# Attention in a two-layer hybrid block: each unit's output is read out of PSUM in the next unit's opening, added in place, with a second buffer for its scale

## The chip, the cores and the metric

The kernel runs on one core of one Trainium2 chip. The metric is the device time of one execution in microseconds (us); lower is better. Everything is fp32; products that need more than one pass of the matrix engine are made from a rounded high part and a remainder (`hi`, `lo`).

## The reference

Two layers work on 1024 latent tokens behind 256 context tokens, width 1024. Each layer normalises the tokens, makes one joint projection, and feeds two mixers: eight heads of latent attention (key width 96, value width 64) and four heads of a gated delta rule in both directions. One output projection and an MLP follow. What matters here is the attention:

```
def mla_attend(q, k, v):
    ...
    def block(qi):
        s = jnp.einsum('bqhd,bkhd->bhqk', qi, k).astype(jnp.float32) * scale
        p = jax.nn.softmax(s, axis=-1).astype(v.dtype)
        return jnp.einsum('bhqk,bkhd->bqhd', p, v)
...
    attn_l = mla_attend(q, jnp.concatenate([kc, k], axis=1), jnp.concatenate([vc, v], axis=1))
    gdn_l, gdn_c = gdn_mix(feat_l, feat_c, gdn_norm_g, not last)
    x = x + g1 * (jnp.concatenate([attn_l, gdn_l], axis=-1) @ w_out)
```

Latent queries read all 1280 keys, context queries the 256 context keys, and the last layer has no context queries.

## The kernel before, in words

Each layer has three stages: projections (`stage1`), the two mixers (`stage2`), and output projection with MLP (`stage3`). `stage2` writes the steps of the delta rule between the attention's units (L801 to L813).

**A unit** is one head, one block of tokens and one half of it, 256 queries: `keys` (L859) lists 40 in layer 0 and 32 in layer 1, 72 in all. Unit i runs the front of query tile i and the back of query tile i-1, interleaved by `PATTERN`.

- `front` computes the scores (names `St`, `S`), copies them out of PSUM with their row maximum (L908), applies the exponential (L926, ScalarE, which also sums the rows), and inverts the two sums of a row (L930, tile `rinv`). The 256 inverted sums lie one per partition; they are needed along the free axis, so a DMA writes them to DRAM (L933) and a second one reads them back, broadcast to 64 partitions (L935, tile `rb`). `rb` has one buffer.
- `back` transposes the exponentials (L955, `pt`), splits them into `ph` (L958, ScalarE) and `pl` (L959, VectorE), and multiplies by the values (L947). The values' high part stands in 64 columns of the weights and their remainder in the other 64, so the product `o` has two halves of 64 partitions that must be added. Tiles `o` alternate between the two halves of one PSUM bank (`o2`, L887).
- At the end of `back` the result is taken out: ScalarE copies the lower half (L969, `oh`), VectorE adds the upper (L971, `ob`), GpSimd multiplies by the inverted sums (L972), and a DMA writes the result to DRAM (L973, tensor `cat`).

**Loads.** `plan` (L861) says in which unit the next head's keys, values and queries are fetched. `prepare(i)`, called as unit i begins, issues these loads through a staging tile `raw` (L834) and splits what the unit before fetched (L839 ScalarE, L841 GpSimd). The splits are put behind `amark`, the last exponential written so far (L879): `issue_after` keeps ScalarE's part of them behind that instruction in ScalarE's order.

**What sets the order.** A scheduler works the program over when it is built: it orders each engine's instructions by written order, priority, and its own estimate of when operands and buffers are ready. All DMAs of this stage are issued by SyncE (SP) from one queue in this order, the loads of the delta rule among them (L1028, L1030, L1032 and L1083). An instruction at the head of an engine's order that has to wait holds up all that stand behind it there.

Of the kernel before, what the change touches and what calls it, by code (L numbers as in the profile page):

```python
# [8 lines left out]
F32 = mybir.dt.float32  # L9
# [3 lines left out]
ALU = mybir.AluOpType  # L13
# [4 lines left out]
P = 128  # L18
# [97 lines left out]
class K:  # L116
# [700 lines left out]
    def attention(self, l, last, ap, psA, psO):  # L817
        nc = self.nc
        ap, ap1, ap2 = ap
# [39 lines left out]
        keys = [(h, b, half) for h in range(H_A) for b in ([1, 2] if last else [0, 1, 2]) for half in range(1 if b == 0 else 2)]  # L859

        plan = {}  # L861
        for h in range(H_A):
            i = min(j for j, k in enumerate(keys) if k[0] == h)
# [5 lines left out]
        wait = []  # L869

        def prepare(i):
            if i == 0:
                for j in sorted(plan):
                    if j < 0:
                        for f, *a in plan[j]:
                            f(*a)()
            todo, wait[:] = list(wait), [f(*a) for f, *a in plan.get(i, [])]
            if todo:
                with self.tc.issue_after(self.amark.ins):  # L879
                    for x in todo:  # L880
                        x()

        state = {}
        self.mark = None


        o2 = psO.tile([P, 2, 256], F32, name="o2")  # L887
        nb = [0]

        def front(h, b, half):  # L890
            prepare(keys.index((h, b, half)))
            t = cur[h]
            qh, ql = cur[h, b]
            nk = NCTX if b == 0 else NT
            nch = (nk + 511) // 512
            sm = self.small.tile([P, 2], F32, tag="sm", name="sm", bufs=3)
            mx = self.small.tile([P, 2, nch], F32, tag=f"mx{nch}", name="mx", bufs=3)
            mn = self.small.tile([P, 2], F32, tag="mn", name="mn", bufs=3)

            def scores(s, i, c0, c1):  # L900
                q = slice(half * 256 + i * P, half * 256 + (i + 1) * P)
                self.mm3(s, qh[:, q], ql[:, q], t["kh"][:, c0:c1], t["kl"][:, c0:c1], True, True)

            pp = [ap.tile([P, NT], F32, tag="p", name="p", bufs=4) for _ in range(2)]

            def keep(i, c, s, c0, c1):

                nc.vector.tensor_scalar(pp[i][:, c0:c1], s, 1.0, None, op0=ALU.mult, op1=ALU.max,  # L908
                                        accum_out=mx[:, i, c:c + 1])


            tail = psA.tile([P, 2, 256], F32, tag="a", name="St")
            for i in range(2):
                scores(tail[:, i, :], i, nk - 256, nk)
            for i in range(2):
                keep(i, nch - 1, tail[:, i, :], nk - 256, nk)
            yield
            for i in range(2):
                for c in range(nch - 1):
                    s = psA.tile([P, 512], F32, tag="a", name="S")  # L920
                    scores(s, i, c * 512, c * 512 + 512)
                    keep(i, c, s, c * 512, c * 512 + 512)
                    if c < nch - 2:
                        yield
                nc.vector.tensor_reduce(mn[:, i:i + 1], mx[:, i, :], op=ALU.max, axis=AX.X, negate=True)
                self.amark = nc.scalar.activation(pp[i][:, :nk], pp[i][:, :nk], AF.Exp, bias=mn[:, i:i + 1],  # L926
                                                  accum_out=sm[:, i:i + 1])
                yield
            r = self.small.tile([P, 2], F32, tag="rinv", name="rinv", bufs=3)
            nc.vector.reciprocal(r, sm)  # L930

            rd = self.dr.tile([2, P], F32, name=f"rinv{l}_{h}_{b}_{half}")
            nc.sync.dma_start(rd.rearrange("i p -> p i"), r)  # L933
            rb = ap2.tile([P, 256], F32, tag="rb", name="rb", bufs=1)
            nc.sync.dma_start(rb[0:64], rd.rearrange("i p -> (i p)").partition_broadcast(64))  # L935
            state[h, b, half] = (pp, rb, nk // P, t["v"])

        def back(h, b, half):
            pp, rb, nkt, v = state.pop((h, b, half))
            q0 = half * 256  # L940
            nb[0] += 1
            o = o2[:, nb[0] % 2, :]
            def pv(k0, ph, pl):
                for i, x in enumerate((ph, pl)):
                    for j in range(2):
                        k = k0 + j
                        nc.tensor.matmul(o, lhsT=v[:, k, :], rhs=x[:, j, :], start=k == 0 and i == 0,  # L947
                                         stop=k == nkt - 1 and i == 1)

            wait = []  # L950
            for k0 in range(0, nkt, 2):
                tp = psA.tile([P, 2, 256], F32, tag="a", name="pt")
                for j in range(2):
                    for i in range(2):
                        self.mark = nc.tensor.transpose(tp[:, j, i * P:(i + 1) * P], pp[i][:, (k0 + j) * P:(k0 + j + 1) * P], self.ident)  # L955
                ph = ap.tile([P, 2, 256], F32R, tag="ph", name="ph", bufs=2)
                pl = ap.tile([P, 2, 256], F32R, tag="pl", name="pl", bufs=2)
                nc.scalar.copy(ph, tp)  # L958
                nc.vector.tensor_tensor(pl, tp, ph.bitcast(F32), op=ALU.subtract)  # L959
                wait.append((k0, ph, pl))  # L960
                if len(wait) > PV_LAG:
                    yield
                    pv(*wait.pop(0))
                yield
            for w in wait:
                pv(*w)
                yield
            oh = ap.tile([P, 256], F32, tag="oh", name="oh", bufs=2)
            nc.scalar.copy(oh[0:64], o[64:128])  # L969
            ob = ap.tile([P, 256], F32, tag="ob", name="ob", bufs=2)  # L970
            nc.vector.tensor_tensor(ob[0:64], o[0:64], oh[0:64], op=ALU.add)  # L971
            nc.gpsimd.tensor_tensor(ob[0:64], ob[0:64], rb[0:64], op=ALU.mult)  # L972
            nc.sync.dma_start(self.cat[h // 2, b][(h % 2) * 64:(h % 2) * 64 + 64, q0:q0 + 256], ob[0:64])  # L973

        units = []
        for i in range(len(keys) + 1):
            def u(i=i):
                f = front(*keys[i]) if i < len(keys) else iter(())
                g = back(*keys[i - 1]) if i else iter(())
                for x in PATTERN:  # L980
                    next(f if x == "f" else g, None)
                for x in (f, g):
                    for _ in x:
                        pass
                return self.mark
            units.append(u)
        return units
# [534 lines left out]
```

## Time and profile before

| | |
|---|---|
| median of 3 runs | 3895.87 us (3893.64 to 3908.26) |
| the profiled execution, its own time | 3909.3 us |
| its span, first to last instruction | 3907.5 us |
| mean granted TensorE clock | 0.940 of full speed |
| PE busy | 3506.5 us (90%) |
| PEld, the weight loads beside PE | 2981.0 us (76%) |
| DVE busy | 2138.5 us (55%) |
| POOL busy | 1518.2 us (39%) |
| ACT busy | 1457.7 us (37%) |

PE is TensorE, DVE VectorE, ACT ScalarE, POOL GpSimd and SPq the queue from which SyncE issues DMAs. Shares are averages over all stages. The mixers of layer 0 run from about 525 to 1080 us of the span, those of layer 1 from about 2600 to 3098 us; "stage" below means these two stretches, together 1053 us.

### The profile page before, as it was taken

To read this page: it belongs to the slowest core of one execution; us is meant where nothing else is said; L and a number is where in the kernel's file an instruction comes from. 1 tells how busy PE (TensorE), PEld (TensorE's weight loads), DVE (VectorE), ACT (ScalarE), POOL (GpSimd) and SP (SyncE) were. 2 spreads that over 40 slices of the span, in tenths; PEclk is the share of its full clock that TensorE was granted. 3 is DMA by queue.
4 is the path that set the end of the run, shared out by engine and by line. 5 is a ranking of instruction groups with operands and counts; after the bars stand their busy time and mean duration, and the time that the engine had idled before them with its cause. 6 is when DMAs were issued, how large, how long until landed. Compare 5 with 4: busy or idle time off the path is not lost.

```text
span 3907.5 us, 52623 instructions
## 1 busy us (share of the span) xinstructions
PE 3506.5 (90%) x19001; PEld 2981.0 (76%) x19001; DVE 2138.5 (55%) x4079; ACT 1457.7 (37%) x3156; POOL 1518.2 (39%) x1359
## 2 busy tenths in 40 slices
PE   8789977989797989999999879878989799999998
PEld 4668767878686878888888667767878688888887
DVE  5157866767579984333334527776767443333334
ACT  4334356666533111112112424346766431222122
POOL 3125865434364222223222313676524342333232
PEclk9899989999798999999999989988999899999999
DMA  5343465455453352111111334456665511111111
GB/s 187 92 135 113 141 151 117 111 94 96 87 189 113 122 186 67 34 43 44 38 38 44 102 101 116 149 134 136 102 112 84 144 43 44 55 49 49 44 54 55
DMA packets 335894, 372.55 MB, mean 95 GB/s; under 512 B 126848, under 2 KB 226576, under 8 KB 333968
## 3 DMA queue, kind: packets, MB, share of 16 engines
q1 hardware_dynamic: 335632, 369.18, 36.5%
q8 instruction: 150, 2.46, 0.3%
q14 instruction: 112, 0.92, 0.1%
HBM read 280.65 MB, written 88.42 MB: 94 GB/s over the span
## 4 chain that ended last, share of the span: by engine, by line
PE 54%; DMA 15%; DVE 13%; issue 5%; ACT 4%; POOL 3%; SPq 1%; DVEq 0%; POOLq 0%; ACTq 0%
PE f2ps L313 6%; PE f2ps L314 6%; PE f2ps L315 6%; PE fps L314 6%; PE fps L315 6%; PE fps L313 6%; DVE adaj L272 3%; PE o L947 2%; PE g L1014 2%; DVE A L1457 2%; PE pt L955 2%; DVE cacc L444 2%; DMA adaw<-w_adaT 2%; DMA rinv<-rinv 2%; PE mm L313 1%
## 5 line engine op out<-in xcount | busy, mean ns | idle before, releaser
L308 POOL TENSOR_TENSOR wlo<-wraw,whi 128x1024 fp32r<-128x1024 f32 (+1 forms) x190 | 462.9, 2445 | 1216.3 <-ACT whi L307 1194.2
L1334 DVE SCALAR_TENSOR_TENSOR x<-f2ps,mod,x 128x512 f32<-128x512 f32 (+1 forms) x648 | 440.6, 689 | 354.1 <-PE f2ps L315 354.0
L307 ACT CAST whi<-wraw 128x1024 fp32r<-128x1024 f32 (+1 forms) x190 | 195.5, 1046 | 1015.7 <-PE f2ps L314 691.8
L313 PE MATMUL f2ps<-ah,whi 128*128 128x512 f32 (+1 forms) x1296 | 474.3, 371 | 33.1 <-DVE x L1334 28.7
L314 PE MATMUL f2ps<-al,whi 128*128 128x512 f32 (+1 forms) x1296 | 478.8, 370 | 1.9 <-DVE al L1323 1.9
L315 PE MATMUL f2ps<-ah,wlo 128*128 128x512 f32 (+1 forms) x1296 | 477.8, 370 | 0.0
L313 PE MATMUL fps<-hh,whi 128*128 128x512 f32 (+1 forms) x1288 | 471.6, 369 | 5.8 <-ACT hh L351 5.8
L314 PE MATMUL fps<-hl,whi 128*128 128x512 f32 (+1 forms) x1288 | 475.8, 370 | 0.5 <-DVE hl L352 0.5
L315 PE MATMUL fps<-hh,wlo 128*128 128x512 f32 (+1 forms) x1288 | 474.8, 369 | 0.0
L1323 DVE TENSOR_TENSOR al<-relu,ah 128x256 fp32r<-128x256 f32 (+1 forms) x161 | 112.7, 706 | 513.0 <-POOL relu L1322 513.0
L313 PE MATMUL mm<-hh,whi 128*128 128x512 f32 (+1 forms) x880 | 333.0, 380 | 30.2 <-ACT craw L430 17.8
L314 PE MATMUL mm<-hl,whi 128*128 128x512 f32 (+1 forms) x880 | 331.8, 377 | 4.5 <-POOL hl L357 2.2
L315 PE MATMUL mm<-hh,wlo 128*128 128x512 f32 (+1 forms) x880 | 327.9, 374 | 1.8 <-POOL wlo L308 1.8
L313 PEld LDWEIGHTS f2ps<-ah,whi 128*128 128x128 f32 x1296 | 248.4, 192 | 75.6 <-DVE x L1334 31.1
L959 DVE TENSOR_TENSOR pl<-pt,ph 128x512 fp32r<-128x512 f32 x328 | 221.0, 686 | 109.7 <-ACT ph L958 101.4
L314 PEld LDWEIGHTS f2ps<-al,whi 128*128 128x128 f32 x1296 | 248.7, 192 | 41.4 <-DVE al L1323 2.1
L313 PEld LDWEIGHTS fps<-hh,whi 128*128 128x128 f32 x1288 | 244.3, 190 | 46.1 <-ACT hh L351 6.2
L315 PEld LDWEIGHTS f2ps<-ah,wlo 128*128 128x128 f32 x1296 | 248.4, 192 | 39.8
L314 PEld LDWEIGHTS fps<-hl,whi 128*128 128x128 f32 x1288 | 245.3, 190 | 40.6 <-DVE hl L352 0.8
L315 PEld LDWEIGHTS fps<-hh,wlo 128*128 128x128 f32 x1288 | 245.0, 190 | 40.0
L955 PE MATMUL pt<-ctab,p 128*128 128x128 f32 x1312 | 220.3, 288 | 57.4 <-DVE p L908 23.2
L1322 POOL TENSOR_TENSOR relu<-relu 128x256 f32<-128x256 f32 (+1 forms) x161 | 159.1, 993 | 227.8 <-ACT ah L1321 227.6
(287 smaller groups left out, 7489.2 us busy)
## 6 DMA issues: line engine op xcount, KB each, us to landing
wraw<-w_ff SPq DMA_DIRECT2D x128, 512.0 KB
adaw<-w_adaT SPq DMA_DIRECT2D x160, 256.0 KB
wraw<-w_in SPq DMA_DIRECT2D x40, 512.0 KB
QK<-QK SPq DMA_DIRECT2D x72, 256.0 KB
A<-A SPq DMA_DIRECT2D x40, 256.0 KB
v<-vtd SPq DMA_DIRECT2D x40, 256.0 KB
kt<-ktd SPq DMA_DIRECT2D x40, 256.0 KB
kT<-kTd SPq DMA_DIRECT2D x36, 256.0 KB
```

Of the source, the lines that this page charges most:

```text
L272: nc.vector.tensor_tensor_reduce(out=j, in0=w, in1=self.sc_b[v][:, s], op0=ALU.mult, op1=ALU.add, scale=1.0, scalar=acc if i else self.bad ...
L307: nc.scalar.copy(hi[:, :n], raw[:, :n])
L308: nc.gpsimd.tensor_tensor(lo[:, :n], raw[:, :n], hi[:, :n].bitcast(F32), op=ALU.subtract)
L313: then(mm(ps, lhsT=lh, rhs=rh, start=start, stop=False))
L314: then(mm(ps, lhsT=lh, rhs=rl, start=False, stop=False))
L315: then(mm(ps, lhsT=ll, rhs=rh, start=False, stop=stop))
L444: nc.vector.scalar_tensor_tensor(a, r[:, o0 + j:o0 + j + nn], cw[:, m * 5 + j:m * 5 + j + 1], a, op0=ALU.mult, op1=ALU.add)
L955: self.mark = nc.tensor.transpose(tp[:, j, i * P:(i + 1) * P], pp[i][:, (k0 + j) * P:(k0 + j + 1) * P], self.ident)
L959: nc.vector.tensor_tensor(pl, tp, ph.bitcast(F32), op=ALU.subtract)
L1322: nc.gpsimd.tensor_tensor(r[:, :n], r[:, :n], r[:, :n], op=ALU.mult)
L1323: nc.vector.tensor_tensor(lo[:, c], r[:, :n], hi[:, c].bitcast(F32), op=ALU.subtract)
L1334: nc.vector.scalar_tensor_tensor(xs, ps[:, :n], g2, xs, op0=ALU.mult, op1=ALU.add)
```

## The change

A unit's result is no longer written at the end of its `back`. It is kept as a function in a list `results`; the next unit's `prepare` runs it ahead of the splits, inside the same `issue_after`, so that ScalarE's copy stands behind the last exponential written. In the last two units the list is emptied at the unit's end. The sum goes into `oh` itself and the tile `ob` is gone, and `rb` gets a second buffer, since it is now read a unit later.

```
-            todo, wait[:] = list(wait), [f(*a) for f, *a in plan.get(i, [])]
+            todo, wait[:] = results + wait, [f(*a) for f, *a in plan.get(i, [])]
+            results.clear()
             if todo:
                 with self.tc.issue_after(self.amark.ins):
                     for x in todo:
...
+        results = []
...
-            rb = ap2.tile([P, 256], F32, tag="rb", name="rb", bufs=1)
+            rb = ap2.tile([P, 256], F32, tag="rb", name="rb", bufs=2)
...
-            oh = ap.tile([P, 256], F32, tag="oh", name="oh", bufs=2)
-            nc.scalar.copy(oh[0:64], o[64:128])
-            ob = ap.tile([P, 256], F32, tag="ob", name="ob", bufs=2)
-            nc.vector.tensor_tensor(ob[0:64], o[0:64], oh[0:64], op=ALU.add)
-            nc.gpsimd.tensor_tensor(ob[0:64], ob[0:64], rb[0:64], op=ALU.mult)
-            nc.sync.dma_start(self.cat[h // 2, b][(h % 2) * 64:(h % 2) * 64 + 64, q0:q0 + 256], ob[0:64])
+
+            def result():
+                oh = ap.tile([P, 256], F32, tag="oh", name="oh", bufs=2)
+                nc.scalar.copy(oh[0:64], o[64:128])
+                nc.vector.tensor_tensor(oh[0:64], o[0:64], oh[0:64], op=ALU.add)
+                nc.gpsimd.tensor_tensor(oh[0:64], oh[0:64], rb[0:64], op=ALU.mult)
+                nc.sync.dma_start(self.cat[h // 2, b][(h % 2) * 64:(h % 2) * 64 + 64, q0:q0 + 256], oh[0:64])
+
+            results.append(result)
...
+
+                if i >= len(keys) - 1:
+                    while results:
+                        results.pop(0)()
                 return self.mark
```

Line numbers in the changed kernel are higher: by 1 or 2 up to L944, by 4 for the copy L969, and by 9 from `delta` on.

The built programs differ on every engine. The same 72 copies, sums, products and DMAs are there; of the 72 copies on ACT, counted from the start of ACT's order, 37 stand at the same place, 16 earlier and 19 later, none by more than 21 places. What moves in nearly every unit is the read `rb` on SP, which comes earlier. Here is SP around the inverted sums of one unit (layer 1, head 2, block 1, second half), before:

```order
L933 DMA rinv1_2_1_1_24856<-rinv_24854 128x2x1
L834 DMA raw_24877<-vd_1_19558 128x128
L1083 DMA qT_25804<-qTd_1_19552 128x512
L1083 DMA v_25808<-vtd_1_19554 128x512
L834 DMA raw_24881<-qd_1_19557 96x512
L834 DMA raw_25127<-qd_1_19557 96x512
L1083 DMA qT_25816<-qTd_1_19552 128x512
L1030 DMA A32_22996<-A1_1_1_21394 32x4x32
L1028 DMA B1_22994<-B1_1_22094 32x8x64 x3
L935 DMA rb_24858<-rinv1_2_1_1_24856 64x256
L973 DMA cat1_1_1_22980<-ob_24870 64x256
```

and in the changed kernel, where the write is L935 and the read L937:

```order
L935 DMA rinv1_2_1_1_24808<-rinv_24806 128x2x1
L1039 DMA A32_22956<-A1_1_1_21354 32x4x32
L834 DMA raw_24823<-vd_1_19518 128x128
L937 DMA rb_24810<-rinv1_2_1_1_24808 64x256
L1092 DMA qT_25744<-qTd_1_19512 128x512
L834 DMA raw_24827<-qd_1_19517 96x512
L1039 DMA A32_22956<-A1_1_1_21354 32x4x32
L834 DMA raw_25071<-qd_1_19517 96x512
L976 DMA cat1_1_1_22940<-oh_24829 64x256
```

Ten DMAs stood between the write of the sums and their read; now two do, and the loads of queries (`raw<-qd`), `qT` and `A32` stand behind the read. Counted over the 72 units, 5.7 DMAs stand between the two on average before (4 units with none), 1.4 after (18 units with none). In two places of the changed kernel a second write stands ahead of the first one's read.

On ACT the copy out of PSUM has other waits (in brackets: the semaphores that an instruction waits for; PE, DVE and Pool are engines, DMAHW is a DMA's landing). Around one unit's copy (layer 0, head 4), before:

```order
L958 CAST ph_7455<-pt_7450 128x512 [waits DVE_49,PE_49]
L926 ACTIVATE p_7368,sm_7364<-p_7368,mn_7366 128x1280 [waits DVE_49]
L839 CAST qh_7354<-raw_7356 96x512 [waits DMAHW7_49,Pool_49]
L969 COPY oh_7473<-o2_4364 64x256 [waits PE_49]
L926 ACTIVATE p_7660,sm_7657<-p_7660,mn_7659 128x256 [waits DVE_49]
```

and in the changed kernel:

```order
L960 CAST ph_7437<-pt_7432 128x512 [waits DVE_49,PE_49]
L928 ACTIVATE p_7350,sm_7346<-p_7350,mn_7348 128x1280 [waits DVE_49]
L839 CAST qh_7331<-raw_7333 96x512 [waits DMAHW0_49]
L973 COPY oh_7631<-o2_4364 64x256 [waits DMAHW1_49,PE_49,Pool_49]
L928 ACTIVATE p_7641,sm_7638<-p_7641,mn_7640 128x256 [waits DVE_49]
```

The copy has not moved here, but where it waited for PE alone (70 of 72 copies before), it now also waits until the buffer's earlier content has been written out (59 of 72 wait for a DMA): `oh` is now the tile that the DMA to `cat` reads.

## Rows read from the trace of the kernel before

**Rows 1.** Busy us (x count) of PE, PEld, DVE, ACT, POOL by stretch; clock, DMA share, GB/s.

```profile
525.00:775.00 250.00, 206.59 (x1492) 186.21 (x1490) 159.61 (x452) 162.94 (x408) 130.24 (x196) 0.91 0.58 119
775.00:1080.00 305.00, 250.11 (x1694) 224.07 (x1693) 194.73 (x558) 183.38 (x437) 111.17 (x110) 0.89 0.55 95
2600.00:2800.00 200.00, 166.75 (x1196) 149.05 (x1197) 126.42 (x361) 134.57 (x319) 123.92 (x197) 0.89 0.65 122
2800.00:3098.00 298.00, 252.73 (x1809) 227.61 (x1808) 203.32 (x565) 188.17 (x441) 105.29 (x100) 0.92 0.56 99
```

**Rows 2.** Waits of SP, 525 to 775 us: in total us, times, longest.

```profile
SPq L935 <- DMA rinv<-rinv: 21.9, 5, 7.4
```

**Rows 3.** Waits of SP, 775 to 1080 us.

```profile
SPq L935 <- DMA rinv<-rinv: 128.8, 17, 8.9
```

**Rows 4.** Waits of SP, 2600 to 3098 us.

```profile
SPq L935 <- DMA rinv<-rinv: 120.1, 19, 9.3
```

**Rows 5.** Timeline of SP, pieces of 740 to 832 us: start, us, instruction.

```profile
752.29 0.39 SPq L933 DMA_DIRECT2D rinv<-rinv  x1
...
760.76 0.45 SPq L935 DMA_DIRECT2D rb<-rinv  x1
...
802.80 0.54 SPq L933 DMA_DIRECT2D rinv<-rinv  x1
803.43 0.45 SPq L834 DMA_DIRECT2D raw<-qd  x1
...
812.91 0.45 SPq L935 DMA_DIRECT2D rb<-rinv  x1
813.42 0.59 SPq L973 DMA_DIRECT2D cat<-ob  x1
```

**Rows 6.** Chain of waits in order of time, 800 to 870 us: start, us, what.

```profile
836.04 9.14 DMA rinv<-rinv
845.25 4.05 DMA rb<-rinv
849.44 0.73 POOL ob L972
850.19 11.72 DMA raw<-vd
```

**Rows 7.** DMA issues, 525 to 1080 us, first and last of 31 rows.

```profile
v<-vtd SPq DMA_DIRECT2D x20, 256.0 KB
...
gng<-gng SPq DMA_DIRECT2D x1, 0.5 KB
```

**Rows 8.** DMA issues, 2600 to 3098 us, first and last of 28 rows.

```profile
kt<-ktd SPq DMA_DIRECT2D x18, 256.0 KB
...
both<-A SPq DMA_DIRECT2D x1, 128.0 KB
```

**Rows 9.** Chain of waits, shares of 525 to 775 us by line.

```profile
by line: DMA cat<-ob 8.1%; PE g L1014 8.0%; DMA rb<-rinv 7.7%; DMA rinv<-rinv 7.0%; issue 6.2%; DVE U L1046 5.4%; PE o L947 5.2%; PE pt L955 4.9%; DMA both<-A 3.8%; DMA qT<-qTd 3.5%; ACT p L926 3.3%; PE S L313 2.2%; DMA B<-B 2.2%; PE S L315
```

**Rows 10.** Chain of waits, shares of 775 to 1080 us by line.

```profile
by line: DMA raw<-vd 10.3%; PE o L947 9.5%; DMA rinv<-rinv 9.2%; DMA craw<-catg 7.5%; PE g L1014 7.2%; DMA craw<-cat 7.1%; PE pt L955 6.4%; issue 3.8%; DMA raw<-qd 3.6%; DVE pl L959 3.1%; DMA rb<-rinv 2.8%; DVE p L908 2.4%; ACT ph L958 2.3%
```

**Rows 11.** Tile ob: its product on POOL; then why its engines sat idle (us, times).

```profile
L972 POOL TENSOR_TENSOR ob<-ob,rb x72: 715/725/1168, 554.3 to 3096.2; 64x256 f32<-64x256 f32 x72
...
  DMA rb<-rinv: 84.4, 17
...
  ACT oh L969: 36.5, 12
...
  DMA cat<-ob: 8.9, 4
```

**Rows 12.** Waits of all engines, 525 to 1080 us.

```profile
PE o L947 <- ACT ph L958: 30.5, 10, 11.9
...
ACT v L839 <- DMA raw<-vd: 25.6, 4, 9.5
```

## The prediction

> **What bounds the kernel now.** I read the busy time by stretch first. PE is busy for 876 of the 1053 us of the two mixer stages, 82 to 85% in each stretch, at 0.89 to 0.92 of the full clock [rows 1]. So PE is the nearest to a bound, with some 177 us in which it waits, and no other engine comes near it. A change to the result's way out, which PE does not compute, can pay only through those waits.
>
> The waits then tell who holds PE up. In layer 0 its dearest one is for the splits on ACT (30.5 us in 10 times), and ACT's own are for loads: the split of the values alone waited 25.6 us for their staging DMA, in 4 times [rows 12]. These loads are all issued by SP, so I read SP's waits third. There stands the largest number near this change: in 41 of the 72 units SP stood before the read of the inverted sums (L935) until their write (L933) had landed, 21.9 us, 128.8 us and 120.1 us, 270.8 in all [rows 2 to 4]. While it stands there it issues nothing else.
>
> The timeline of SP shows what one such wait is made of. From the issue of the write to that of the read it took 8.5 us (752.29 to 760.76), 10.1 us (802.80 to 812.91) [rows 5] and 9.2 us (836.04 to 845.25) [rows 6]; I use their mean, 9.3 us. Two neighbouring issues start 0.5 to 0.6 us apart [rows 5]; I use 0.6. The read then needs another 4 us, GpSimd multiplies, and the next load of values comes behind that on the chain [rows 6]. Both this round trip on SP and the product's wait on POOL are thus already part of what ends last, in places.
>
> **The change, part by part.**
>
> *Work.* Nothing is added or removed: 72 copies, sums, products and DMAs stay, in the same shapes. The in-place sum writes as many elements as before. I cost all of this at nothing.
>
> *The place of the copy and the sum.* The lists of instructions show that "one unit later" is mostly the unit's boundary itself: 37 of 72 copies keep their place on ACT. VectorE stood 36.5 us for that copy, in 12 places [rows 11]; a copy that is queued elsewhere moves this wait, it does not end it, since the product of the matrices that the copy reads ends when it did. I take nothing for it, with 10 us to either side.
>
> *The second buffer of `rb`.* This is the part that moves most. With one buffer, the scheduler could place the read only behind the product of the unit before; 5.7 other DMAs stood between write and read. With two it places it as soon as it believes the write done, with 1.4 DMAs between. For POOL this is a gain: the product waited 84.4 us for `rb`, in 17 places [rows 11]. But what it is worth is read from the chain: in the first stretch of layer 0, `rb` holds 7.7% of 250 us, 19 us, and in the second 2.8% of 305 us, 9 us [rows 9, 10]. Of these 28 us I credit 10: the long gaps between write and read are in the first stretch, and there the read itself still comes a round trip behind the write; in the second the gaps were short before. The bounds are 0 and 28.
>
> For SP it is a loss. The round trip is the same 9.3 us, and there is less to issue inside it. After the write's own 0.6 us and 1.4 more issues, 9.3 - 0.6 - 0.8 = 7.9 us of standing remain, in 70 of 72 units (two writes go ahead of an earlier read, and share one round trip): 553 us in place of 270.8, so 282 us more. What is queued behind is everything that the stage loads: queries, keys and values, and the delta rule's operands.
>
> What of this reaches the end? Two counts bound it. The lower: how long SP must take if it waits for nothing else. In layer 0 the DMA issues of 525 to 1080 us sum to 434 over all rows of that view [rows 7], 10.9 for each of 40 units; a unit then costs SP 9.3 + (10.9 - 1 - 1.4) x 0.6 = 14.4 us, 576 us in all against 555 now. In layer 1 they sum to 389 [rows 8], 12.2 for each of 32 units; 9.3 + (12.2 - 2.4) x 0.6 = 15.2 us, 486 against 498. So layer 0 would be at least 21 us longer, and layer 1 would have no slack worth the name; SP, which I had not counted among the engines, becomes a second bound. The upper: nothing is absorbed, 282 us.
>
> To choose between them I compare, in the trace, how much of SP's standing is on the chain. In 775 to 1080 us the write's landing holds 9.2% of the chain, 28 us [rows 10], of 128.8 us of standing [rows 3], 22%. In 525 to 775 us, where SP has more to issue, it holds 7.0%, 17.5 us [rows 9], of 21.9 [rows 2], 80%. The new standing falls largely in the first stretches, but there SP also waits for other things that would shrink. I take a quarter of 282, 70 us, nearer the 22% since that rests on more units.
>
> *A rule on that price.* The Trainium skill ("DMA: Bandwidth & Descriptors", section "Anatomy of one DMA — SWDGE (gpsimd) path") puts a DMA's fixed cost, setup and completion, at about 2.0 us, measured on GpSimd's path. By it the write would be done before 1.4 issues have passed and SP would hardly stand at all; the sum would be POOL's credit alone, an estimate near 3886 us. The trace does not agree: the three round trips above took 8.5 to 10.1 us on SP's queue, so I keep 9.3.
>
> *ACT's new wait.* The copy on ACT now also waits until the DMA to `cat` of two units earlier has landed, since that DMA reads `oh`; 59 of 72 copies wait for a DMA where none did. Before, the sum on VectorE waited for it, 8.9 us in 4 places [rows 11]. Behind the copy on ACT are the splits and exponentials for which PE waits. If the DMA is as early as it was, this is half of 8.9 us on the chain, 4.5; if SP's standing delays it, each unit may lose more: this is the case below.
>
> **Sum.** +70 (SP) - 10 (POOL) + 5 (ACT) = +65 us. The profiled execution took 3909.3 us by its own time, so it would be 3974; it lies 13.4 us over the median of the three runs, 3895.87, so I forecast **3961 us**.
>
> **The rivals.**
>
> *Faster: SP's standing stays slack.* The place is the first units of each layer; the price is POOL's wait on the chain, up to 28 us, and the part of VectorE's wait for the copy that is on the chain, at most 10. It decides if the loads behind the read are issued 8 us or more before they are needed. For it: in 775 to 1080 us SP already stood 128.8 us, and 78% of that was off the chain. Against it: layer 0's count of 576 us for SP exceeds the stage. Time: 3896 - 28 - 10 = 3858, or any part of it down to -20. Chance 0.21.
>
> *No change: the change does not do what it says.* Half of the copies keep their place, the credit and a small loss on SP cancel, and what is left is the scheduler's shuffling of neighbours. A measurement of this kernel can tell about 0.5%, 19 us, from no change. For it: layer 1's count stays below its stage. Time 3877 to 3915. Chance 0.19.
>
> *Slower by SP alone*, the forecast: 3915 to 4010, from +20 (the lower count) to 40% of 282. Chance 0.45.
>
> *Much slower: ACT stops for the DMA to `cat`.* SP issues that DMA behind a standing of 7.9 us, it lands some us later, ACT stands before the copy, PE before the splits, and with PE's gaps its clock falls. It decides if the DMA lands later than two units (28 us) after its copy. At one standing of 7.9 us in every fourth of the 59 copies it costs 117 us more: 4078. Chance 0.15.
>
> **How the numbers follow.** The last two are slower than the bound of 0.5%: 0.60. Faster 0.21, within it 0.19. The range leaves out the better half of the first rival and the worse half of the last: 3870 to 4060, the forecast's own being 3915 to 4010.
>
> **What would show it.** Right: SP's standing before the read of the inverted sums grows from 271 us in 41 units to 450 us or more in over 60; the product's wait for `rb` on POOL falls below 84 us, to about half; both stages are longer, layer 0's by more, and the first stretch of each most; ACT's waits for the staging DMAs grow, PE's waits for ACT's splits with them. The rest of the kernel, from 1215 to 2300 us and behind 3200, keeps its lengths within a few us. Wrong: SP's standing grows as counted and the stages do not lengthen, so that it was slack; or it does not grow, because the round trip is shorter when fewer loads are ahead of the write. If the copy on ACT shows waits for the DMA to `cat` of more than 30 us, it is the last rival.

## The result and the profile after

The changed kernel takes 3959.22 us, median of 4 runs (3956.09 to 3968.95), against 3902.07 for the kernel before in the same comparison (3893.64 to 3908.89): ratio 1.0154, 95% interval 1.0127 to 1.018: 57 us slower by the medians, 60 by the ratio. The profiled execution took 3958.21 us.

The busy times of the whole span are the same; only the span is 49 us longer. First the page's first part, of the changed kernel:

```profile
PE 3514.6 (89%) x19001; PEld 2987.5 (76%) x19001; DVE 2133.1 (54%) x4079; ACT 1457.9 (37%) x3156; POOL 1520.1 (38%) x1359
```

The 49 us are all between the start of layer 0's mixers and the end of layer 1's. These rows are ACT's copies out of PSUM in the view of tile `oh`, first and last start of each layer; before:

```profile
L969 ACT COPY oh<-o x40: 350/369/372, 529.5 to 1075.5; 64x256 f32<-64x256 f32 x40
L969 ACT COPY oh<-o x32: 368/369/372, 2617.5 to 3095.1; 64x256 f32<-64x256 f32 x32
```

and of the changed kernel:

```profile
L973 ACT COPY oh<-o x40: 363/368/371, 535.7 to 1104.8; 64x256 f32<-64x256 f32 x40
L973 ACT COPY oh<-o x32: 368/368/373, 2649.0 to 3144.2; 64x256 f32<-64x256 f32 x32
```

Layer 0's last copy starts 29 us later (1075.5 to 1104.8), and from there to layer 1's last takes 20 us more (2019.6 to 2039.4).

Busy time by stretch, of the changed kernel (columns as in [rows 1]):

```profile
525.00:775.00 250.00, 202.23 (x1427) 181.34 (x1426) 149.16 (x436) 155.26 (x388) 128.53 (x194) 0.88 0.54 115
775.00:1108.00 333.00, 258.28 (x1754) 231.58 (x1754) 198.32 (x573) 189.57 (x453) 111.86 (x111) 0.87 0.41 88
2640.00:2840.00 200.00, 164.01 (x1195) 149.12 (x1195) 124.90 (x355) 128.43 (x311) 114.19 (x178) 0.90 0.50 109
2840.00:3147.00 307.00, 251.65 (x1766) 225.99 (x1765) 199.53 (x551) 186.18 (x437) 105.32 (x100) 0.89 0.46 95
```

PE is busy for 876 us in these stretches, as before; their length went from 1053 to 1090 us. So PE does the same work with longer gaps. The loss is spread over the stage: by 775 us PE had run 1427 instructions, 65 fewer than before [rows 1], some 11 us at that stretch's pace. A unit's progress shows it too. The sums of layer 0's eighteenth unit, the first that are inverted behind 775 us in both kernels, come 14 us late, about half of the 29; before and after:

```profile
782.42 0.16 DVE L930 RECIPROCAL rinv<-sm 128x2 f32<-128x2 f32 x1
...
796.65 0.17 DVE L932 RECIPROCAL rinv<-sm 128x2 f32<-128x2 f32 x1
```

The waits over the whole span, of the changed kernel, one engine each (SP, POOL, PE, ACT):

```profile
SPq L937 <- DMA rinv<-rinv: 514.9, 68, 9.7
...
POOL oh L975 <- DMA rb<-rinv: 53.7, 9, 12.1
...
PE o L949 <- ACT ph L960: 131.5, 21, 16.8
...
ACT v L839 <- DMA raw<-vd: 68.2, 10, 17.2
...
ACT oh L973 <- DMA cat<-oh: 36.5, 6, 11.3
```

SP's standing before the read went from 270.8 us in 41 units [rows 2 to 4] to 514.9 us in 68. POOL's wait for `rb` fell from 84.4 [rows 11] to 53.7. PE's wait for the splits doubled, from 67.3 us over the span before to 131.5, and ACT's wait for the values went from 42.9 us to 68.2. The two before:

```profile
PE o L947 <- ACT ph L958: 67.3, 17, 13.4
...
ACT v L839 <- DMA raw<-vd: 42.9, 8, 13.2
```

One link of that, in the timeline of SP in the changed kernel:

```profile
803.74 1.07 SPq L1092 DMA_DIRECT2D kt<-ktd  x2
804.91 0.38 SPq L935 DMA_DIRECT2D rinv<-rinv  x1
805.38 0.89 SPq L1092 DMA_DIRECT2D QK<-QK  x2
814.95 0.47 SPq L937 DMA_DIRECT2D rb<-rinv  x1
815.51 0.54 SPq L834 DMA_DIRECT2D raw<-vd  x1
```

and the same moment in its chain of waits:

```profile
804.91 10.03 DMA rinv<-rinv
814.95 0.47 SPq L937
815.51 4.12 DMA raw<-vd
820.79 0.59 ACT ph L960
821.43 0.80 PE o L949 x2
```

SP stands 8.6 us before the read with the values' load behind it; the load lands after that, ACT splits, and PE goes on. Over layer 0's second stretch, 775 to 1108 us, these are the shares of the chain now:

```profile
by line: DMA rinv<-rinv 18.0%; PE o L949 9.6%; DMA cat<-oh 9.0%; PE pt L957 7.1%; PE g L1023 6.9%; issue 5.7%; DMA raw<-vd 3.6%; DMA raw<-qd 3.2%; DMA craw<-cat 3.1%; DMA craw<-catg 3.1%; DVE pl L961 2.7%; PE S L313 2.4%; PE S L315 2.4%; PE
```

The write's landing held 9.2% before, the load of the values 10.3%, and the DMA to `cat` was not among the shares of 2.3% and more [rows 10]. So the loads are not all that SP's standing holds up: the result's own write, which is issued behind it, now holds 9.0% of this stretch.

### The profile page after: what moved, and what is told of

Same layout as the page of the kernel before. It is cut to its first block, busy times and chain, and to the rows that moved or that the text cites. A ratio compares the mean times of both kernels' runs of the same rounds, so it can differ in the third digit from the quotient of the medians.

```text
span 3956.4 us, 52667 instructions
## 1 busy us (share of the span) xinstructions
PE 3514.6 (89%) x19001; PEld 2987.5 (76%) x19001; DVE 2133.1 (54%) x4079; ACT 1457.9 (37%) x3156; POOL 1520.1 (38%) x1359
## 4 chain that ended last, share of the span: by engine, by line
PE 54%; DMA 13%; DVE 13%; issue 5%; ACT 4%; POOL 3%; SPq 1%; POOLq 0%; DVEq 0%; ACTq 0%
PE f2ps L313 6%; PE f2ps L314 6%; PE f2ps L315 6%; PE fps L314 6%; PE fps L313 6%; PE fps L315 6%; DVE adaj L272 3%; DMA rinv<-rinv 3%; PE g L1023 3%; PE o L949 3%; DVE cacc L444 2%; PE pt L957 2%; DVE A L1466 2%; DMA adaw<-w_adaT 2%; DMA cat<-oh 1%
## 5 line engine op out<-in xcount | busy, mean ns | idle before, releaser
L949 PE MATMUL o<-ph,v 128*128 128x256 f32 x656 | 157.0, 323 | 131.8 <-ACT ph L960 131.5
```

## The experiments

Theory A: the second buffer lets the scheduler place the read close behind the write, SP stands for the round trip, and the loads queued behind it come late. Rival B: the in-place sum makes ACT wait for the DMA to `cat`. Rival C: the later place of the result costs the time. The first four kernels separate the three edits. Two need one buffer for `oh` in place of two, since a second `rb` has no room in SBUF beside two `oh` and two `ob`.

**e1: two buffers for `rb` alone.** On the kernel before:

```
-            rb = ap2.tile([P, 256], F32, tag="rb", name="rb", bufs=1)
+            rb = ap2.tile([P, 256], F32, tag="rb", name="rb", bufs=2)
...
-            oh = ap.tile([P, 256], F32, tag="oh", name="oh", bufs=2)
+            oh = ap.tile([P, 256], F32, tag="oh", name="oh", bufs=1)
```

> The kernel before with a second buffer for rb alone (and one for oh instead of two, for room). The result stays at the unit's end, the sum stays in ob. Its order has 1.6 DMAs between the write of the inverted sums and their read, as the changed kernel (1.4; before 5.7). Theory A, the read placed close behind the write makes SP stand: 3950 +- 15 us, SP's standing there 500 us in about 68 units. Rival B, the copy on ACT waits for the DMA to cat: 3902 +- 10, since no copy waits for a DMA here. Rival C, the later place of the result costs it: 3902 +- 10.

Measured: 3983.92 us, ratio 1.0178 (1.0161 to 1.0195). The buffer alone is as slow as the whole change, or slower, and slower than A had it: 3950 +- 15 us over the 3902.07 from which it was reckoned is 1.0084 to 1.0161. The waits of its SP:

```profile
SPq L935 <- DMA rinv<-rinv: 535.5, 66, 10.8
```

**e2: the sum in place alone.** On the kernel before:

```
-            ob = ap.tile([P, 256], F32, tag="ob", name="ob", bufs=2)
-            nc.vector.tensor_tensor(ob[0:64], o[0:64], oh[0:64], op=ALU.add)
-            nc.gpsimd.tensor_tensor(ob[0:64], ob[0:64], rb[0:64], op=ALU.mult)
+            nc.vector.tensor_tensor(oh[0:64], o[0:64], oh[0:64], op=ALU.add)
+            nc.gpsimd.tensor_tensor(oh[0:64], oh[0:64], rb[0:64], op=ALU.mult)
```

> The kernel before with the sum written in place alone: rb has one buffer, the result stays at the unit's end. 5.2 DMAs between write and read; 62 of 72 copies on ACT wait for a DMA. Theory A: 3902 to 3915 us, SP's standing about 290 us. Rival B: 3935 to 3960, with ACT's copy waiting 30 us or more for cat and PE's wait for the splits up by as much. Rival C: 3902.

Measured: 3908.85 us, ratio 0.9992 (0.9978 to 1.0006). No difference that can be told. SP stands longer than the 290 us foretold. The waits of its SP and of its ACT:

```profile
SPq L935 <- DMA rinv<-rinv: 334.6, 49, 10.0
...
ACT oh L969 <- DMA cat<-oh: 11.4, 3, 5.1
```

ACT does wait for `cat` here, in 3 places, and no loss comes of it that can be told.

**e3: the result's later place alone.** The changed kernel with `rb` back to one buffer and the sum back in `ob`:

```
-            rb = ap2.tile([P, 256], F32, tag="rb", name="rb", bufs=2)
+            rb = ap2.tile([P, 256], F32, tag="rb", name="rb", bufs=1)
...
+                ob = ap.tile([P, 256], F32, tag="ob", name="ob", bufs=2)
+                nc.vector.tensor_tensor(ob[0:64], o[0:64], oh[0:64], op=ALU.add)
```

> The changed kernel with one buffer for rb and the sum in ob, as before: only the result's place is new. 5.5 DMAs between write and read, no copy on ACT waits for a DMA. Theory A: 3902 +- 12 us, SP's standing about 275 us. Rival B: the same. Rival C: 3940 to 3960.

Measured: 3888.38 us, ratio 0.9939 (0.9916 to 0.9962): this part makes the kernel faster, which no theory had expected. SP's standing stays as before:

```profile
SPq L937 <- DMA rinv<-rinv: 284.8, 44, 10.4
```

**e4: later place and two buffers, no in-place sum.** The changed kernel with the sum in `ob` and one buffer for `oh`.

> The changed kernel with the sum in ob again (one buffer for oh, for room): later place and two buffers for rb, no in-place sum. 1.4 DMAs between write and read, no copy on ACT waits for a DMA. Theory A: 3945 +- 15 us, SP's standing 500 us. Rival B: 3902 +- 12. Rival C: 3945 as well, so that e3 tells A from C.

Measured: 3973.53 us, ratio 1.0149 (1.0131 to 1.0167), the whole loss without any wait of ACT's copy for a DMA, at the upper end of A's 1.0072 to 1.0149. The waits of its SP and of its VectorE:

```profile
SPq L937 <- DMA rinv<-rinv: 538.7, 67, 10.4
...
DVE ob L975 <- DMA cat<-ob: 31.8, 5, 10.6
```

As the cause, B falls by e2 (the in-place sum alone costs nothing) and e4 (the loss is there without it), C by e3. But the wait for the DMA to `cat` on which B rests is not gone in e4: with the sum in `ob`, VectorE's sum takes it over, 31.8 us (33.6 in e1, 8.9 before [rows 11]). It is long only where SP stands long, so a late write of the result is one of the ways in which the standing may cost time; what it costs beside the late loads was not separated. Between e3 and e4 the main edit is the second buffer (with one `oh` fewer): 2.1% of the time.

**e5: the read held back, both buffers kept.** On the changed kernel, the read is written into the next unit and put on SP behind the DMA to `cat` of the unit before:

```
+            rb = ap2.tile([P, 256], F32, tag="rb", name="rb", bufs=2)
+            with ExitStack() as q:
+                if self.catm is not None:
+                    q.enter_context(self.tc.issue_after(self.catm.ins))
+                nc.sync.dma_start(rb[0:64], rd.rearrange("i p -> (i p)").partition_broadcast(64))
...
-                nc.sync.dma_start(self.cat[h // 2, b]...
+                self.catm = nc.sync.dma_start(self.cat[h // 2, b]...
```

> The changed kernel with the read of the inverted sums held on SP behind the DMA to cat of the unit before; two buffers for rb, the in-place sum and the later place of the result all stay. 6.0 DMAs between write and read (changed kernel 1.4, before 5.7); 62 copies on ACT wait for a DMA, as in the changed kernel. Theory A (the read's place on SP is the cost): ratio to before 0.990 to 1.002, SP's standing at the read 250 to 330 us, PE's wait for the splits back to about 65 us. Rival D (two buffers cost something else, such as the transfer's own time or the room): ratio 1.012 to 1.018 with SP's standing gone all the same.

Measured: 3893.84 us, ratio 0.9942 (0.9922 to 0.9961). All three edits are in, and the loss is gone; what is left is e3's gain. The waits of its SP and of its PE:

```profile
SPq L944 <- DMA rinv<-rinv: 206.7, 41, 8.4
...
SPq L979 <- POOL oh L978: 107.9, 40, 9.0
...
PE o L952 <- ACT ph L963: 64.2, 16, 14.2
```

PE's wait for the splits is back at 64.2 us, as A had it. SP now stands 107.9 us for the product before `cat` as well, so its two waits add up to 314.6 us; yet the kernel is as fast as e3. How long SP stands is thus not by itself the price.

**e7: a read that need not wait.** On the changed kernel:

```
-            nc.sync.dma_start(rb[0:64], rd.rearrange("i p -> (i p)").partition_broadcast(64))
+            nc.sync.dma_start(rb[0:64], self.scd[0, 0:256].partition_broadcast(64))
```

> The changed kernel whose read of rb takes 256 numbers from another tensor that has long been in DRAM, so that it need not wait for the write of the inverted sums; the write stays, the result is scaled by the wrong numbers. Same number and size of DMAs on SP. Theory A: SP's standing at the read is 0, ratio 0.975 to 0.995, below e3's 0.994 if part of the 271 us before was on the chain. Rival E (the two DMAs themselves, their packets and issue, are the cost, not the waiting): ratio 1.010 to 1.018.

Measured: 3868.3 us, ratio 0.9878 (0.9857 to 0.9899). The wait of its SP at the read:

```profile
SPq L937 <- DMA rinv<-rinv: 1.9, 1, 1.9
```

Same DMAs, same sizes; with this wait gone the changed kernel is 2.7% faster. So it is the wait, not the two DMAs. SP's waits for the write's landing are not all gone: the trace puts 84.7 us down to it before other DMAs, which do not read the sums (none in the changed kernel), and why is not shown. POOL's wait for `rb` went with SP's, from 53.7 us to 9.3, so the 2.7% holds both. From e5 to e7 it is 0.6%, some 25 us: what SP's 206.7 us at the read and POOL's 79.0 us for `rb` still cost, together, where the read is held back.

**e6: no round trip, the scale put into the transpose.** On the changed kernel, with the sum in `ob` and one buffer for `oh`:

```
+                nc.vector.reciprocal(r[:, i:i + 1], sm[:, i:i + 1])
+                nc.vector.tensor_scalar(dg[:, i, :], self.ident, r[:, i:i + 1], None, op0=ALU.mult)
...
-                        self.mark = nc.tensor.transpose(tp[...], pp[i][...], self.ident)
+                        self.mark = nc.tensor.matmul(tp[...], lhsT=pp[i][...], rhs=dg[:, i, :], start=True, stop=True)
```

The write to DRAM, the read and the product by `rb` are taken out.

> No round trip at all: the transposes multiply by a diagonal of the inverted sums instead of the identity, so the exponentials come out scaled; the write, the read and the product on POOL are gone (144 DMAs fewer on SP, 72 products fewer on POOL), 144 small products of 128x128 on VectorE are new. Result's later place kept, sum in ob. Theory A: SP's 271 us of standing before go, and what of them was on the chain with them, 22% or more, about 60 us, and POOL's 84 us of waiting for rb; VectorE gets some 30 us of work, and the transposes now wait for the sum's inverse and the product, about 0.5 us in each unit, 36 us if nothing hides it. Ratio 0.975 to 0.992. If SP's standing before was slack and only what the second buffer added was not: 0.992 to 1.003.

Measured: 3854.62 us, ratio 0.9839 (0.9819 to 0.9859), faster than both kernels. Its busy time by stretch:

```profile
525.00:775.00 250.00, 241.33 (x1884) 225.09 (x1884) 183.07 (x538) 174.42 (x430) 127.94 (x188) 0.98 0.46 128
775.00:1040.00 265.00, 255.03 (x1964) 238.06 (x1963) 204.99 (x589) 171.43 (x410) 85.17 (x77) 1.00 0.32 90
2570.00:2770.00 200.00, 195.25 (x1557) 182.37 (x1556) 150.92 (x422) 141.29 (x336) 108.74 (x169) 0.99 0.46 126
2770.00:3040.00 270.00, 266.54 (x2075) 250.84 (x2074) 205.89 (x581) 177.47 (x418) 88.81 (x77) 1.00 0.32 91
```

PE is busy for 97% of the stage: its waits are nearly gone, and PE has become the bound. Part of that is new work. These are the transposes in the views of tile `pt` or their line, before:

```profile
L955 PE MATMUL pt<-ctab,p x1312: 270/273/477, 522.1 to 3082.6; 128*128 128x128 f32 x188
```

and in e6:

```profile
L954 PE MATMUL pt<-dg,p x2624: 270/275/583, 524.1 to 3033.3; 128*128 128x128 f32 x188
```

The product with a diagonal takes two matmul instructions where the transpose takes one, 1312 more in all.

**e8: the sums spread by TensorE.** This keeps the transposes. On the changed kernel, in place of write and read:

```
+            rp = psA.tile([P, 2, 256], F32, tag="a", name="rp")
+            for i in range(2):
+                nc.tensor.matmul(rp[0:64, 0, i * P:(i + 1) * P], lhsT=r[:, i:i + 1].to_broadcast([P, 64]),
+                                 rhs=self.ident, start=True, stop=True)
+            rb = ap2.tile([P, 256], F32, tag="rb", name="rb", bufs=2)
+            nc.scalar.copy(rb[0:64], rp[0:64, 0, :])
```

> The changed kernel with the inverted sums spread by TensorE: two products of the sums, repeated over 64 columns, with the identity put them along the free axis in a PSUM tile, and ACT copies that to rb; write and read through DRAM are gone, the transposes stay as they were. New: 4 short matmul instructions (about 0.11 us of issue each, 32 us in all) and one copy of 0.37 us on ACT (27 us in all) in each of 72 units; 144 DMAs fewer. Theory A: SP's standing is gone, and PE has 1312 transposing instructions less than in e6, which was held by PE (95 to 100% busy in its stages): ratio 0.960 to 0.984, at or below e6's 0.984. If the PSUM tile that this takes from the scores' four costs a wait in each unit: 0.984 to 0.995.

Measured: 3830.82 us, ratio 0.978 (0.9763 to 0.9797), the fastest of all, 2.2% below the kernel before. Its busy time by stretch:

```profile
525.00:1040.00 515.00, 469.84 (x3308) 418.94 (x3308) 365.51 (x1007) 354.83 (x871) 236.95 (x301) 0.94 0.38 106
2560.00:3040.00 480.00, 443.87 (x3199) 395.01 (x3198) 337.52 (x942) 339.62 (x801) 239.74 (x313) 0.97 0.41 115
```

and the waits of its PE over the span:

```profile
PE rp L936 <- DVE rinv L932: 40.5, 31, 6.5
...
PE o L951 <- ACT ph L962: 13.4, 10, 8.1
```

PE's wait for the splits is down to 13.4 us from 67.3. The next price is in the first row: PE, in order, stands at the new product for the inverted sums.

## Why the prediction was right, point by point

**What bounds the kernel.** Held: PE's work in the stages did not change, and what changed are its waits. One reading was selective: in layer 0 ACT waited as long for PE before its copies `ph` (27.2 us for the product `o`, 26.7 for the transposes) as for the load of the values (25.6). SP as a second bound was not tested alone. In layer 0 of the changed kernel its standing at the read (85.7 and 193.4 us) and 431 issues at 0.6 us make 538 of the 583 us from 525 to 1108: near the bound, not above it.

**SP's standing.** Counted: 553 us in 70 units, 282 more than before. Measured: 514.9 us in 68, 244 more. The round trip of 9.3 us held: over all 72 units of the changed kernel it took 9.2 us in the mean, 7.4 to 12.1, from the issue of the write to that of the read. Its price was sized at a quarter, 70 us, less the 10 credited to POOL. The runs give these two only together: 70 us for 265 us more standing at the read from before to e1 (ratio 1.0178), 82 for 254 from e3 to e4 (0.9939 to 1.0149), 83 for 308 from e5 to the changed kernel (0.9942 to 1.0154), 26 to 32%. So the quarter was about right, and 60 us were 10 to 23 too few. The upper count, all of 282, was far off.

**The later place.** This is the term that was mis-sized: taken at 0 with 10 us to either side, measured by e3 at -0.6%, -24 us (-15 to -33). With two buffers it brings less: from e1 to e4 (1.0178 to 1.0149) some -11 us (-20 to -2), which is hardly told from -24. The argument was that a wait for the product that the copy reads is only moved. Over the span VectorE's wait for the copy fell little, from 36.5 us to 30.1 in e3, and POOL's wait for `rb` from 84.4 to 78.7. Which of its moved instructions brings the gain was not tried, nor whether it is more than the scheduler's new order of neighbours; the cause stays open.

**The in-place sum.** Taken at +5, measured at -0.1% (-0.2 to +0.1%). The changed kernel does show 36.5 us of ACT's copy waiting for the DMA to `cat`, above the 30 us that were named as the sign of the last rival. The sign did not point to this edit: e4, without it, is as slow, and the wait stands on VectorE there.

**POOL's credit.** Taken at -10. POOL's wait fell by 31 us, less than the half that was foretold (84.4 to 53.7). The second buffer does not explain that fall: it took the wait from 78.7 to 77.6 us between e3 and e4, and from 84.4 to 71.8 in e1.

**The sum.** +65 us against some 60 measured (1.27 to 1.8%). It is nearer than its terms: the second buffer cost 70 to 82 us where 60 were taken, and the later place gave back 11 to 24 where nothing was taken. That these two errors nearly cancel is luck. That the loss comes from SP's standing, at a quarter to a third of its length, is not: e5 and e7 show it.

**Where in the stage.** Foretold: layer 0 more than layer 1, which held (29 and 20 us); the rest of the kernel unchanged, which held (the whole span grew by the same 49 us); and the first stretch of each most, which failed. Layer 0 lost 11 to 14 of its 29 us in its first stretch, about what that stretch's share of the time would give. SP's standing grew by as much in both stretches of layer 0 (21.9 to 85.7 us, and 128.8 to 193.4). The share of the standing that was on the chain before, 80% in the first stretch and 22% in the second, thus did not tell what more of it would cost: all parts of the change together, it is at most 14 us in the first and at least 15 in the second.

**The rule on a DMA's fixed cost.** The Trainium skill's 2.0 us ("DMA: Bandwidth & Descriptors", "Anatomy of one DMA — SWDGE (gpsimd) path") would have left SP next to no standing. The prediction has the write done before 1.4 issues have passed; with 0.6 us for its own issue and 0.8 for those, an estimate by that figure is 0.6 us of standing in each unit, 42 us in 70. The round trips of 8.5 to 10.1 us before, and the standings of up to 9.7 us in the changed kernel, decide against it for this path and this pattern of 256 scattered numbers.

## What to carry to other kernels

A second buffer is not free where a scheduler orders a queue by its own estimate of a DMA's time: it may place a read right behind the write that it depends on, and everything behind on that queue then waits out the round trip. Look in such a queue for pairs of dependent DMAs and count what stands between them; hold the reader back behind later issues, or better, take the pair off the queue, as e8 does with four short matmul instructions for each unit. Before judging a change of several edits, run each alone: here one was worth -0.6%, one nothing, and one +1.8% by itself, while all three together are +1.5%.

## What was not expected of the hardware

The write of 256 inverted sums, 1 KB in all, took as long as loads of many times its size: 9.14 us in [rows 6] and 10.03 in the changed kernel's chain, where a load of 64 KB (`raw<-vd`) took 11.72 and 4.12 us. What of that is the write itself and what the traffic beside it was not tried.

The granted clock went with the gaps. In the mixer stages it was 0.89 to 0.92 with PE busy 82 to 85% [rows 1], 0.87 to 0.90 in the changed kernel, 0.94 and 0.97 in e8 with PE busy 91 and 92%, and 0.98 to 1.00 in e6, where PE was busy 97%; so between the two levels of 1.2 and 2.4 GHz nearly all of e6's stage was at the upper. e6 gains although its PE is busy for 958 us in these stretches, against 876 before. How much of the gain is the clock and how much the waits was not measured apart.
